# gMLP mixer of a fused encoder step: v turned into rows on VectorE and through DRAM instead of on TensorE, and weight chunks fetched one chunk further ahead

## Chip, cores, metric

One core of one Trainium2 chip runs the whole step in one launch. The metric is the device time of that launch in microseconds (us); the kernel before has a median of 1330.05 us.

## What is computed

Two layers of macaron form run on 256 prompt frames and 32 sample frames (288 columns in all), model width 1024. Every layer is half a SwiGLU feed-forward, a mixer, and half a feed-forward. The mixer of layer 1 is the chunked gMLP that the change touches:

```python
def _mixer_c(h, w_in, ln_g, ln_b, w_s, b_s, w_out):
    u, v = jnp.split(jax.nn.gelu(h @ w_in), 2, axis=-1)      # 2048 channels each
    v = _layernorm(v, ln_g, ln_b)                            # over the channels
    ...
    mixed = jnp.einsum('gij,bnjgc->bnigc', ws, vg) + b_s...  # over the 128 frames of a chunk, 8 groups
    return (u * mixed.reshape(B, T, D_C)) @ w_out, v
```

All operands are float32.

## The kernel before

**Layout.** Activations lie with channels on the partitions and the 288 frames along the free axis (32 sample frames first). The weights stream from DRAM as chunks of up to 1024 rows by 256 columns (1 MB), in the order in which they are used. `fetch` (L180) loads a chunk into one of three `wraw` buffers through SP's queue. `pieces` splits it in four pieces of two 128-row blocks: ScalarE casts the high part `wh` (L207) and VectorE subtracts to get the low part `wl` (L208). The `wh` and `wl` tiles hold four half chunks each, so a chunk is split while the chunk ahead of it multiplies. `mm` then runs, for each row block and each half of the 256 columns, three products of 288 columns (L247 with `wl`, L248 and L249 with `wh`): 48 products for a chunk of eight blocks. The first product of a block is the one that reads `wl`.

**Queues.** `next_chunk` issues the fetches ahead and `tick` hands out the pieces and the work of "lanes" (side work, at a rate per row block). The Tile layer then schedules: it may move an instruction later or earlier on its engine while the program is built, and what it leaves is a fixed order on each engine. On the chip every engine works through its own order; an instruction that waits holds up all behind it on that engine.

**The mixer, `mixer_c`.** Eight v chunks (called v0 to v7 here), then eight u chunks (u0 to u7), then the output projection in eight chunks (o0, o1, ...). A chunk's two accumulators are evacuated by VectorE (L296), which multiplies by the norm; the accumulators are two pairs, so the chunk after next needs the evacuation. ScalarE then applies the gelu (L992 and L994 for v, L1089 for u).

- `tokens(n, v)` turns a v chunk so that frames lie on the partitions: four 128x128 transposes on TensorE (L975) into PSUM and one copy by ScalarE (L976) into `vt`. After every second chunk the sample's part `vs` is turned too (L981, L982), and VectorE takes the statistics of 512 channels of `vt` (L984).
- `statistics` joins them (L1008 to L1016) and takes the power on GpSimd (L133). `normed` scales `vt` and `vs` in nine steps on VectorE (L1025).
- `spatial(n)` multiplies `vt` of chunk n by the spatial weights on TensorE (L1050 for the sample, L1069), finishes on VectorE (L1057 to L1082), and `put` writes the product with u as high part `hh` (ScalarE, L316) and low part `hl` (VectorE, L317). `u` has four buffers, so u4 can be evacuated only when u0 is done.
- The projection reads `hh` and `hl`: its first chunk o0 needs u0 to u3, o1 needs u4 to u7.

Of the kernel before, what the change touches and what calls it, by code (L numbers as in the profile page):

```python
# [14 lines left out]
P = 128  # L15
D = 1024
KD = D // P
TP = 256
TS = 32
# [12 lines left out]
WIN = ((32, 160), (160, 288), (0, 128))  # L32
# [61 lines left out]
class Net:  # L94
# [4 lines left out]
    def __init__(self, tc, ctx, I, O):  # L99
        self.tc, self.nc, self.I, self.O = tc, tc.nc, I, O  # L100
        e = ctx.enter_context
        self.const = e(tc.tile_pool(name="const", bufs=1))
        self.wraw = e(tc.tile_pool(name="wraw", bufs=3))
        self.wspl = e(tc.tile_pool(name="wspl", bufs=4))
        self.acc = e(tc.tile_pool(name="acc", bufs=2, space=PSUM))
        self.misc = e(tc.tile_pool(name="misc", bufs=4, space=PSUM))
        self.nrm = e(tc.tile_pool(name="nrm", bufs=1))
        self.stream, self.pos = [], 0
        self.raw, self.spl = {}, {}
        self.uid = 0  # L110
        self.ahead = None
        self.lanes = []
        self.lv = None
        self.nlane = Lane(self.NORM_RATE)
# [38 lines left out]
    def to_cols(self, name, b, x, xs):  # L153

        pt = self.ps(name)
        for i in range(2):
            self.nc.tensor.transpose(pt[:, i * P:i * P + P], x[:, i], self.ident)
        if b == 0:
            self.nc.tensor.transpose(pt[:, TP:TP + P], xs, self.ident)
        return pt  # L160

    def both(self, x):

# [48 lines left out]
    def next_chunk(self):  # L212
        i = self.pos
        self.pos += 1
        for _ in self.ahead or self.pieces(i):
            pass
        for j in (i + 1, i + 2):
            self.fetch(j)
        self.ahead = self.pieces(i + 1)
        self.rate = -(-self.blocks(i + 1) // self.PIECE) / self.blocks(i)  # L220
        self.due = 0.999
        self.raw.pop(i)
        return self.spl.pop(i)
# [686 lines left out]
    def mixer_c(self, gnext):  # L910
        nc, I, O = self.nc, self.I, self.O
# [3 lines left out]
        with self.tc.tile_pool(name="c", bufs=1, reuse_waits="tile") as pool:  # L915
            self.hidden(pool, 16)
            T = lambda tag, shape, bufs=None: self.t(pool, shape, tag, bufs=bufs)
# [4 lines left out]
            J = N // 2  # L922
            vt, vs, vc = T("vt", [P, 2, DC]), T("vs", [P, J, P]), T("vc", [P, J, P])
            st = T("st", [P, 3, 4, 6])
# [28 lines left out]
            def row_sums():  # L953
# [6 lines left out]
                for a, e in ((0, 3), (3, 6), (6, 8)):  # L960
# [4 lines left out]
                    nc.scalar.copy(out=rs[:, a:e], in_=pt[:, :n].rearrange("p (g i) -> p g i", i=P + TS))  # L965
                    yield

            def tokens(n, v):
                yield
                pv = self.ps("vt")  # L970
                for w in range(2):
                    for b in range(2):
                        s, e = WIN[w]
                        a = 256 * w + P * b
                        nc.tensor.transpose(pv[:, a:a + P], v[:, b, s:e], self.ident)  # L975
                nc.scalar.copy(out=vt[:, :, n * 256:n * 256 + 256], in_=pv.rearrange("p (w c) -> p w c", w=2))  # L976
                yield
                if n % 2:
                    j = n // 2
                    pv = self.ps("vs")  # L980
                    nc.tensor.transpose(pv[:, :P], vc[:, j], self.ident)  # L981
                    nc.scalar.copy(out=vs[:, j], in_=pv[:, :P])  # L982
                    for w in range(2):
                        nc.vector.bn_stats(st[:, w, j], vt[:, w, (n - 1) * 256:(n + 1) * 256])  # L984
                    yield

            spw = spatial_weights()
            next(spw)
# [14 lines left out]

            def statistics():
                mv = state["mv"] = T("mv", [P, 3, 2])

                sp = T("sp", [P, 6])
                nc.vector.bn_stats(sp, vs.rearrange("p j c -> p (j c)"))  # L1008
# [19 lines left out]

            def sample_out():

                gb, bb, y = (T(n, [P, J, P]) for n in ("lng", "lnb", "vo"))
                for to, name in ((gb, "c_ln_g"), (bb, "c_ln_b")):
                    for k in range(4):
                        nc.gpsimd.dma_start(out=to[TS * k:TS * k + TS], in_=I[name][0].rearrange(
# [334 lines left out]
```

## Time and profile before

| what | us |
|---|---|
| median of three runs (1329.81, 1330.05, 5818.11) | 1330.05 |
| the profiled execution | 1330.23 |
| its span, first to last instruction | 1328.5 |
| TensorE busy in it (PE) | 1322.6 |
| VectorE busy (DVE) | 878.4 |
| ScalarE busy (ACT) | 672.7 |

The profile follows one execution. PE is TensorE's products, PEld its weight loads, DVE VectorE, ACT ScalarE, POOL GpSimd, SP the engine that issues most transfers; a q behind a name is that engine's instruction queue. Lines (L247) are those of the kernel before. A product's duration is modelled and overlaps the next one, so the pace of TensorE is read from the starts. 1330.23 less 1328.5 leaves 1.7 us outside the span.

### The profile page before, as it was taken

How to read it: one execution, taken by the hardware profiler on the slowest of the kernel's cores; microseconds unless marked ns; L12 is line 12 of the kernel's file. 1: busy time of each engine (PE TensorE's matmuls, PEld its weight loads, DVE VectorE, ACT ScalarE, POOL GpSimd, SP SyncE). 2: the span in 40 equal slices, each digit the busy share in tenths (PEclk: the TensorE clock that was granted, in tenths of full speed). 3: DMA queues.
4: the chain of work that ended last, by engine and by line, in shares of the span. 5: the costliest groups of instructions: out<-in, count | busy, mean ns of one | idle time of the engine just before them, and what ended most of it. 6: DMA issues, size and time to landing. Idle time of an engine off the chain costs nothing.

```text
span 1328.5 us, 24573 instructions
## 1 busy us (share of the span) xinstructions
PE 1322.6 (100%) x9986; PEld 1316.6 (99%) x9986; DVE 878.4 (66%) x1682; ACT 672.7 (51%) x1381; POOL 43.6 (3%) x67
## 2 busy tenths in 40 slices
PE   9999999999999999999999999999999999999998
PEld 9999999999999999999999999999999999999998
DVE  7666556879787866666555766655568966665653
ACT  7544445474747466544444644444565445444432
POOL 1000000010111010000000000020000000000000
PEclk9999999999999999999999999999999999999999
DMA  8555455453544346555545555575544545555443
GB/s 282 178 178 168 144 175 186 154 161 108 165 135 136 113 135 199 159 159 162 175 148 183 159 169 167 173 191 178 164 155 131 163 159 159 164 167 178 151 129 105
DMA packets 221907, 214.70 MB, mean 162 GB/s; under 512 B 12385, under 2 KB 221074, under 8 KB 221794
## 3 DMA queue, kind: packets, MB, share of 16 engines
q1 hardware_dynamic: 221010, 211.20, 50.7%
q0 software_dynamic: 624, 1.77, 0.6%
q8 instruction: 78, 1.28, 0.4%
q14 instruction: 35, 0.29, 0.1%
q10 hardware_dynamic: 160, 0.17, 0.1%
HBM read 208.27 MB, written 4.85 MB: 160 GB/s over the span
## 4 chain that ended last, share of the span: by engine, by line
PE 98%; DMA 1%; DVE 0%; SPq 0%; issue 0%; ACT 0%; DVEq 0%
PE acc L249 30%; PE acc L248 30%; PE acc L247 30%; PE sc L612 1%; DMA wraw<-in_ffn_w_up_dram 1%; PE sp L1069 1%; PE S L685 0%; PE zs L822 0%; PE sc L640 0%; PE ob L889 0%; PE vt L975 0%; PE kt L141 0%; PE z L834 0%; PE ob L884 0%; DVE wl L208 0%; SPq L190 0%
## 5 line engine op out<-in xcount | busy, mean ns | idle before, releaser
L207 ACT CAST wh<-wraw 128x512 fp32r<-128x512 f32 x768 | 441.9, 619 | 475.6 <-PE acc L249 358.3
L208 DVE TENSOR_TENSOR wl<-wraw,wh 128x512 fp32r<-128x512 f32 x768 | 508.0, 688 | 260.9 <-ACT wh L207 260.1
L247 PE MATMUL acc<-xh,wl 128*128 128x288 f32 x2096 | 629.1, 300 | 0.0
L249 PE MATMUL acc<-xh,wh 128*128 128x288 f32 x2096 | 618.6, 295 | 0.0
L248 PE MATMUL acc<-xl,wh 128*128 128x288 f32 x2096 | 618.5, 295 | 0.0
L248 PEld LDWEIGHTS acc<-xl,wh 128*128 128x128 f32 x2096 | 394.1, 188 | 0.5
L247 PEld LDWEIGHTS acc<-xh,wl 128*128 128x128 f32 x2096 | 393.9, 188 | 0.6
L249 PEld LDWEIGHTS acc<-xh,wh 128*128 128x128 f32 x2096 | 393.5, 188 | 0.0
L247 PE MATMUL acc<-hh,wl 128*128 128x288 f32 x960 | 284.7, 297 | 0.0
L248 PE MATMUL acc<-hl,wh 128*128 128x288 f32 x960 | 283.4, 295 | 0.0
L249 PE MATMUL acc<-hh,wh 128*128 128x288 f32 x960 | 283.1, 295 | 0.0
L247 PEld LDWEIGHTS acc<-hh,wl 128*128 128x128 f32 x960 | 180.2, 188 | 0.8 <-ACT hh L866 0.2
L248 PEld LDWEIGHTS acc<-hl,wh 128*128 128x128 f32 x960 | 180.3, 188 | 0.2
L249 PEld LDWEIGHTS acc<-hh,wh 128*128 128x128 f32 x960 | 180.3, 188 | 0.0
L296 DVE TENSOR_TENSOR u<-acc,rb 128x576 f32<-128x576 f32 x52 | 39.4, 757 | 49.1 <-PE acc L249 49.1
L296 DVE TENSOR_TENSOR g<-acc,rb 128x576 f32<-128x576 f32 x47 | 35.6, 758 | 46.6 <-PE acc L249 46.6
L316 ACT CAST hh<-u 128x576 fp32r<-128x576 f32 x52 | 35.1, 676 | 55.2 <-DVE u L442 40.4
L317 DVE TENSOR_TENSOR hl<-u,hh 128x576 fp32r<-128x576 f32 x52 | 39.4, 759 | 7.7 <-ACT hh L316 1.7
L323 ACT ACTIVATE xh<-xT,cols 128x288 fp32r<-128x288 f32 x40 | 21.3, 532 | 26.5 <-DVE xT L391 15.4
L442 DVE TENSOR_TENSOR u<-u,g 128x576 f32<-128x576 f32 x44 | 33.1, 753 | 0.0
L440 ACT ACTIVATE g<-g 128x576 f32<-128x576 f32 x44 | 30.0, 681 | 0.1
L324 DVE SCALAR_TENSOR_TENSOR xl<-xT,cols,xh 128x288 fp32r<-128x288 f32 x40 | 20.6, 516 | 8.5 <-ACT xh L323 8.5
(315 smaller groups left out, 777.6 us busy)
## 6 DMA issues: line engine op xcount, KB each, us to landing
wraw<-in_ffn_w_up_dram SPq DMA_DIRECT2D x44, 1024.0 KB, 6.0
wraw<-in_ffn_w_gate_dram SPq DMA_DIRECT2D x43, 1024.0 KB, 5.4
wraw<-in_ffn_w_down_dram SPq DMA_DIRECT2D x32, 1024.0 KB, 5.3
wraw<-in_ab_w_in_dram SPq DMA_DIRECT2D x28, 1024.0 KB, 5.2
wraw<-in_c_w_in_dram SPq DMA_DIRECT2D x16, 1024.0 KB, 5.4
wraw<-in_ffn_w_down_dram SPq DMA_DIRECT2D x16, 768.0 KB, 4.5
wraw<-in_c_w_out_dram SPq DMA_DIRECT2D x8, 1024.0 KB, 5.3
wraw<-in_ab_w_out_dram SPq DMA_DIRECT2D x8, 768.0 KB, 4.4
```

What stands on the lines that cost most here:

```text
L207: self.nc.scalar.copy(out=h[:, x], in_=w[:, a:b])
L208: self.nc.vector.tensor_tensor(out=l[:, x], in0=w[:, a:b], in1=h[:, x].bitcast(F32), op=ALU.subtract)
L247: mm(o, lhsT=l[:, k, c], rhs=hi[:, r], start=st, stop=False)
L248: mm(o, lhsT=h[:, k, c], rhs=lo[:, r], start=False, stop=False)
L249: mm(o, lhsT=h[:, k, c], rhs=hi[:, r], start=False, stop=en)
L296: self.nc.vector.tensor_tensor(out=x, in0=acc[:, :, :NT], in1=self.rb, op=ALU.mult)
L316: nc.scalar.copy(out=hh, in_=h)
L317: nc.vector.tensor_tensor(out=self.hl[:, k:k + 2], in0=h, in1=hh.bitcast(F32), op=ALU.subtract)
L323: nc.scalar.activation(out=self.xh[:, k], in_=x, func=AF.Copy, scale=g)
L324: nc.vector.scalar_tensor_tensor(out=self.xl[:, k], in0=x, scalar=g, in1=self.xh[:, k].bitcast(F32), op0=ALU.mult, op1=ALU.subtract)
L440: nc.scalar.activation(out=g, in_=g, func=AF.Silu)
L442: nc.vector.tensor_tensor(out=u, in0=u, in1=g, op=ALU.mult)
```

## The change

The transposes of a v chunk leave TensorE. VectorE transposes blocks of 32x32 inside two instructions of 128x256 per chunk, into a tile of 128x512 that shares a buffer with `lnb` or `vo`. Four transfers (one for each 32 partitions) write it to a scratch in DRAM in runs of 32 floats, which puts the blocks in their places; two transfers read it back into `vt`, 128x2x128 each. ScalarE's copy goes away. The statistics of 512 channels are taken one chunk later (the last in `statistics`). `next_chunk` also fetches chunk i + 3; `wraw` still has three buffers.

```diff
@@ class Net
+        self.rows = e(tc.tile_pool(name="rows", bufs=2, space=bass.MemoryType.DRAM))
...
+    def to_rows(self, y, x):
+
+        nc = self.nc
+        n = y.shape[1]
+        for i, e in x:
+            nc.vector.transpose(y[:, i:i + e.shape[1]], e)
+        rows = self.t(self.rows, [n, P], "rows")
+        to = rows.rearrange("(n t) (a c) -> a t n c", t=TS, a=4)
+        for q in range(4):
+            nc.sync.dma_start(out=to[q], in_=y[TS * q:TS * q + TS].rearrange("t (n c) -> t n c", c=TS))
+        return rows
...
-        for j in (i + 1, i + 2):
+        for j in (i + 1, i + 2, i + 3):
             self.fetch(j)
@@ mixer_c
+            def means(j):
+                for w in range(2):
+                    nc.vector.bn_stats(st[:, w, j], vt[:, w, 512 * j:512 * j + 512])
+
             def tokens(n, v):
                 yield
-                pv = self.ps("vt")
-                for w in range(2):
-                    for b in range(2):
-                        s, e = WIN[w]
-                        a = 256 * w + P * b
-                        nc.tensor.transpose(pv[:, a:a + P], v[:, b, s:e], self.ident)
-                nc.scalar.copy(out=vt[:, :, n * 256:n * 256 + 256], in_=pv.rearrange("p (w c) -> p w c", w=2))
+                y = T(("lnb", "vo")[n % 2], [P, 2 * TP])
+                rows = self.to_rows(y, [(TP * b, v[:, b, TS:]) for b in range(2)])
+                for b in range(2):
+                    c = n * 256 + b * P
+                    nc.sync.dma_start(out=vt[:, :, c:c + P],
+                                      in_=rows[TP * b:TP * b + TP].rearrange("(w t) c -> t w c", t=P))
                 yield
                 if n % 2:
...
-                    for w in range(2):
-                        nc.vector.bn_stats(st[:, w, j], vt[:, w, (n - 1) * 256:(n + 1) * 256])
-                    yield
+                elif n:
+                    means(n // 2 - 1)
+                yield
...
             def statistics():
                 mv = state["mv"] = T("mv", [P, 3, 2])
+                means(J - 1)
```

The orders below are those of the built programs; lines of the changed kernel are shifted (L309 is the old L296, L220 and L221 are L207 and L208, L1106 is L1089, L330 is L317, L1093 is L1076, L1098 is L1081). Numbers behind a name tell one buffer's use from another.

**Place 1, VectorE from the evacuation of u1 to that of u3.** `wraw_11616` is u3's chunk before, `wraw_11550` after; `wraw_11709` and `wraw_11642` are u4's. Before, with the evacuations of u1 (`acc_11615`) and u2 (`acc_11708`):

```order
L208 TENSOR_TENSOR wl_11718<-wraw_11616,wh_11717 128x512
L1025 TENSOR_SCALAR vt_10878<-vt_10878,mv_11653,pw_11668 128x512 x2
L1025 TENSOR_SCALAR vs_10879<-vs_10879,mv_11653,pw_11668 128x512
L1025 TENSOR_SCALAR vt_10878<-vt_10878,mv_11653,pw_11668 128x512 x2
L296 TENSOR_TENSOR u_11705<-acc_11615,rb_10942 128x576
L1025 TENSOR_SCALAR vt_10878<-vt_10878,mv_11653,pw_11668 128x512 x4
L208 TENSOR_TENSOR wl_11752<-wraw_11616,wh_11751 128x512 x2
L208 TENSOR_TENSOR wl_11803<-wraw_11709,wh_11802 128x512
L1059 TENSOR_TENSOR xs_11764<-sp_11761,cols 128x128
```

After, with the evacuations of u2 (`acc_11739`) and u3 (`acc_11814`):

```order
L309 TENSOR_TENSOR u_11811<-acc_11739,rb_10946 128x576
L168 STREAM_TRANSPOSE vo_11674<-v_11545 128x256 x2
L221 TENSOR_TENSOR wl_11749<-wraw_11550,wh_11748 128x512
L983 BN_STATS st_10885<-vt_10882 128x6 x2
L221 TENSOR_TENSOR wl_11749<-wraw_11550,wh_11748 128x512
L221 TENSOR_TENSOR wl_11784<-wraw_11550,wh_11783 128x512 x2
L309 TENSOR_TENSOR u_11902<-acc_11814,rb_10946 128x576
L221 TENSOR_TENSOR wl_11824<-wraw_11642,wh_11823 128x512 x2
L221 TENSOR_TENSOR wl_11869<-wraw_11642,wh_11868 128x512 x2
L221 TENSOR_TENSOR wl_11915<-wraw_11740,wh_11914 128x512
L983 BN_STATS st_10885<-vt_10882 128x6 x2
```

The split of u3's chunk stood ahead of u2's evacuation and stands behind it now, all four pieces; the split of u4's chunk stands behind u3's evacuation. The transposes of v7 and the last statistics stand there as well.

**Place 1, ScalarE, from the gelu of u0.** Before:

```order
L1089 ACTIVATE u_11601<-u_11601 128x576
L207 CAST wh_11676<-wraw_11527 128x512
L982 COPY vs_10879<-vs_11634 128x128
L207 CAST wh_11717<-wraw_11616 128x512 x2
L207 CAST wh_11751<-wraw_11616 128x512 x2
L1089 ACTIVATE u_11705<-u_11705 128x576
L207 CAST wh_11802<-wraw_11709 128x512 x2
```

After:

```order
L1106 ACTIVATE u_11627<-u_11627 128x576
L220 CAST wh_11690<-wraw_11461 128x512
L998 COPY vs_10883<-vs_11700 128x128
L1106 ACTIVATE u_11736<-u_11736 128x576
L1106 ACTIVATE u_11811<-u_11811 128x576
L220 CAST wh_11748<-wraw_11550 128x512 x2
L220 CAST wh_11783<-wraw_11550 128x512 x2
L1106 ACTIVATE u_11902<-u_11902 128x576
L220 CAST wh_11823<-wraw_11642 128x512 x2
```

The casts of u3's chunk stood ahead of the gelu of u1 and stand behind the gelu of u2 now, those of u4's behind the gelu of u3.

**Place 2, TensorE, the first spatial product.** Before it stands in chunk u2 (`acc_11708`), 36 products into it:

```order
L248 MATMUL acc_11708<-xl,wh_11676 128x288
L249 MATMUL acc_11708<-xh,wh_11676 128x288
L1050 MATMUL sp_11761<-wsB_10886,vs_10879 128x128
L247 MATMUL acc_11708<-xh,wl_11677 128x288
L248 MATMUL acc_11708<-xl,wh_11676 128x288
```

After it stands in chunk u5 (`acc_11994`), 22 products into it, with three more behind it:

```order
L260 MATMUL acc_11994<-xh,wl_11915 128x288
L1067 MATMUL sp_11833<-wsB_10890,vs_10883 128x128
L1086 MATMUL sp_11856<-wsT_10889,vt_10882 128x128 x2
L1086 MATMUL sp_11878<-wsT_10889,vt_10882 128x128 x2
L1086 MATMUL sp_11945<-wsT_10889,vt_10882 128x128 x2
L261 MATMUL acc_11994<-xl,wh_11914 128x288
```

The spatial products of all eight u chunks are moved towards the end of the stage by nearly three chunks.

**Place 2, VectorE, around the last `hl` of the stage.** Before, with u6's (`u_12150`) and u7's (`u_12237`); `wl_12398` is half of o1's first chunk:

```order
L317 TENSOR_TENSOR hl_10877<-u_12150,hh_10876 128x576
L1076 SCALAR_TENSOR_TENSOR x_12328<-sp_12329,cols,z_12332 128x256
L1076 SCALAR_TENSOR_TENSOR x_12328<-sp_12335,cols,z_12338 128x256
L208 TENSOR_TENSOR wl_12398<-wraw_12241,wh_12397 128x512
L1081 TENSOR_TENSOR u_12237<-x_12328,u_12237 128x2x256
L208 TENSOR_TENSOR wl_12398<-wraw_12241,wh_12397 128x512
L317 TENSOR_TENSOR hl_10877<-u_12237,hh_10876 128x576
```

After, with u6's (`u_12173`) and u7's (`u_12263`); `wl_12416` is the first half of o1's first chunk:

```order
L330 TENSOR_TENSOR hl_10881<-u_12173,hh_10880 128x576
L1093 SCALAR_TENSOR_TENSOR x_12364<-sp_12371,cols,z_12374 128x256
L1099 TENSOR_TENSOR u_12263<-xs_12328,u_12263 128x2x32
L1098 TENSOR_TENSOR u_12263<-x_12364,u_12263 128x2x256
L221 TENSOR_TENSOR wl_12416<-wraw_12177,wh_12415 128x512 x2
L330 TENSOR_TENSOR hl_10881<-u_12263,hh_10880 128x576
```

The rows here are much the same as before. Those of all eight u chunks lie between the first spatial product and this place, in a shorter stretch of the program now.

**Place 3, SP's queue around the last rows.** Before, the fetches of u4 to u6 (`wraw_11709` and the two behind it) follow each other with nothing between:

```order
L180 DMA wraw_11616<-in_c_w_in_dram 128x8x256
L180 DMA wraw_11709<-in_c_w_in_dram 128x8x256
L180 DMA wraw_11794<-in_c_w_in_dram 128x8x256
L180 DMA wraw_11883<-in_c_w_in_dram 128x8x256
L1040 DMA out_dram<-vo_11606 128x1x128 x4
```

After (`rows_11604` is v6, `rows_11677` v7; `wraw_11642` is u4's chunk, `wraw_11740` u5's):

```order
L172 DMA rows_11604<-lnb_11601 32x16x32 x4
L193 DMA wraw_11642<-in_c_w_in_dram 128x8x256
L991 DMA vt_10882<-rows_11604 128x2x128 x2
L172 DMA rows_11677<-vo_11674 32x16x32 x4
L193 DMA wraw_11740<-in_c_w_in_dram 128x8x256
L991 DMA vt_10882<-rows_11677 128x2x128 x2
L193 DMA wraw_11815<-in_c_w_in_dram 128x8x256
```

Between two fetches there are now four writes to the scratch and two reads from it, and a read waits for its writes to land. Outside the mixer the orders of TensorE, VectorE, ScalarE and GpSimd are the same rows; on SP a fetch is moved ahead of a small transfer in a few places.

## Rows read from the trace of the kernel before

**Rows 1.** The page: busy time, share and instructions of the engines.

```profile
PE 1322.6 (100%) x9986; PEld 1316.6 (99%) x9986; DVE 878.4 (66%) x1682; ACT 672.7 (51%) x1381; POOL 43.6 (3%) x67
```

**Rows 2.** The page, the chain that ended last: shares by engine.

```profile
PE 98%; DMA 1%; DVE 0%; SPq 0%; issue 0%; ACT 0%; DVEq 0%
```

**Rows 3.** What TensorE's products waited for over the whole span, the longest of them: total us, times, longest.

```profile
PE acc L1144 <- DVE ms L1155: 1.2, 1, 1.2
```

**Rows 4.** TensorE's products in order of time around one set of transposes: start us, us, engine, line, operation, count.

```profile
961.98 0.29 PE L249 MATMUL acc<-xh,wh 128*128 128x288 f32 x1
962.11 0.60 PE L975 MATMUL vt<-ident,v 128*128 128x128 f32 x4
962.47 0.38 PE L247 MATMUL acc<-xh,wl 128*128 128x288 f32 x1
962.68 0.30 PE L248 MATMUL acc<-xl,wh 128*128 128x288 f32 x1
962.82 0.29 PE L249 MATMUL acc<-xh,wh 128*128 128x288 f32 x1
```

**Rows 5.** The weight loads around the first set: the same columns, and in brackets the idle time and what ended it.

```profile
958.03 0.42 PEld L975 LDWEIGHTS vt<-ident,v 128*128 128x128 f32 x4 [0.26 <-ACT v L994]
```

**Rows 6.** VectorE in order of time: u0's evacuation, a stretch of the u chunks, and the last `hl`; columns as in rows 4 and 5. The pace is read from start to start.

```profile
1008.74 0.76 DVE L296 TENSOR_TENSOR u<-acc,rb 128x576 f32<-128x576 f32 x1 [1.24 <-PE acc L249]
...
1019.30 1.91 DVE L1025 TENSOR_SCALAR vt<-vt,mv,pw 128x512 f32<-128x512 f32 x4
1021.12 1.90 DVE L208 TENSOR_TENSOR wl<-wraw,wh 128x512 fp32r<-128x512 f32 x3
1022.93 0.29 DVE L1059 TENSOR_TENSOR xs<-sp,cols 128x128 f32<-128x128 f32 x1
...
1030.25 0.77 DVE L317 TENSOR_TENSOR hl<-u,hh 128x576 fp32r<-128x576 f32 x1
1030.92 0.24 DVE L1082 TENSOR_TENSOR u<-xs,u 128x64 f32<-128x64 f32 x1
1031.05 0.30 DVE L1057 TENSOR_TENSOR zs<-RS,cols 128x128 f32<-128x128 f32 x1
1031.25 0.77 DVE L296 TENSOR_TENSOR u<-acc,rb 128x576 f32<-128x576 f32 x1
1031.92 0.50 DVE L1076 SCALAR_TENSOR_TENSOR x<-sp,cols,z 128x256 f32<-128x256 f32 x1
1032.31 0.70 DVE L208 TENSOR_TENSOR wl<-wraw,wh 128x512 fp32r<-128x512 f32 x1
...
1034.11 0.36 DVE L1073 SCALAR_TENSOR_TENSOR z<-RS,cols,BS 128x128 f32<-128x128 f32 x1
1034.37 0.70 DVE L1081 TENSOR_TENSOR u<-x,u 128x512 f32<-128x512 f32 x1
1034.97 0.37 DVE L1073 SCALAR_TENSOR_TENSOR z<-RS,cols,BS 128x128 f32<-128x128 f32 x1
...
1071.29 0.76 DVE L317 TENSOR_TENSOR hl<-u,hh 128x576 fp32r<-128x576 f32 x1 [0.20 <-ACT hh L316]
```

**Rows 7.** ScalarE, GpSimd and VectorE, groups by line and form from 950 to 1085 us: count | busy us, mean ns of one | idle time ahead of them.

```profile
L207 ACT CAST wh<-wraw 128x512 fp32r<-128x512 f32 x76 | 44.3, 618 | 28.7 <-PE acc L249 22.0 <-issue 6.6
L1089 ACT ACTIVATE u<-u 128x576 f32<-128x576 f32 x8 | 5.5, 686 | 8.5 <-DVE u L296 8.5
...
L133 POOL TENSOR_TENSOR pw<-ve,mhalf 128x3 f32<-128x3 f32 x1 | 1.2, 1244 | 124.8 <-DVE ve L1016 124.8
...
L984 DVE BATCH_NORM_STATS2 st<-vt 128x6 f32<-128x512 f32 x8 | 5.1, 682 | 0.7 <-ACT vt L976 0.7
...
L1012 DVE BATCH_NORM_AGGREGATE mv<-st 128x2 f32<-128x24 f32 x3 | 0.6, 236 | 0.0
```

**Rows 8.** TensorE in order of time, the product that the last `hl` lets start; columns as in rows 4.

```profile
1071.95 0.29 PE L247 MATMUL acc<-hh,wl 128*128 128x288 f32 x1
1072.10 0.40 PE L248 MATMUL acc<-hl,wh 128*128 128x288 f32 x1
```

**Rows 9.** VectorE's transposes of the results (L1307): duration in ns, least, median and most.

```profile
L1307 DVE STREAM_TRANSPOSE sq<-xT x6: 472/472/478, 1269.5 to 1308.8; 128x288 f32<-128x288 f32 x6
```

**Rows 10.** SP's own time to issue the transfers of the results (L1311) and of one output tile (L1040): ns, least, median, most.

```profile
L1311 SPq DMA_DIRECT2D out_dram<-sq x48: 314/434/1401, 1270.0 to 1314.8; - x48
...
L1040 SPq DMA_DIRECT2D out_dram<-vo x4: 588/600/707, 1027.1 to 1029.1; - x4
```

**Rows 11.** Transfers by issue: count, KB each, median us from issue to landing.

```profile
wraw<-in_c_w_in_dram SPq DMA_DIRECT2D x16, 1024.0 KB, 5.4
...
out_dram<-sq SPq DMA_DIRECT2D x24, 32.0 KB, 2.4
```

**Rows 12.** Two windows: length, then busy us (instructions) of PE, PEld, DVE, ACT, POOL, the granted clock, the DMA share and GB/s. The first holds small writes of results alone, the second weight fetches.

```profile
1290.00:1295.00 5.00, 5.00 (x40) 5.00 (x39) 3.30 (x6) 1.46 (x3) 0.00 (x0) 1.00 0.23 37
941.00:947.40 6.40, 6.40 (x51) 6.40 (x50) 4.75 (x9) 4.42 (x10) 0.00 (x0) 1.00 0.53 164
```

**Rows 13.** What SP's queue waited for over the whole span: total us, times, longest.

```profile
SPq L180 <- DVE wl L208: 970.1, 171, 11.0
```

**Rows 14.** Two windows, columns as in rows 12: one of the v chunks, one of the u chunks.

```profile
981.00:987.50 6.50, 6.50 (x51) 6.50 (x50) 3.38 (x6) 3.04 (x7) 0.00 (x0) 1.00 0.55 164
1022.00:1029.00 7.00, 7.00 (x56) 7.00 (x55) 7.00 (x16) 3.32 (x6) 0.00 (x0) 1.00 0.54 163
```

More of the change, by code (lines that the diff above doesn't have):

```diff
@@ L1029, in sample_out @@
             def sample_out():
-                gb, bb, y = (T(n, [P, J, P]) for n in ("lng", "lnb", "vo"))
+                gb, bb, y = (T(n, [P, J * P]).rearrange("p (j c) -> p j c", c=P) for n in ("lng", "lnb", "vo"))
                 for to, name in ((gb, "c_ln_g"), (bb, "c_ln_b")):
```

## Prediction

> **What bounds the kernel now.** I read the page's busy time first: TensorE is busy 1322.6 us [rows 1], all but 6 us of the span. The chain that ended last is TensorE's to 98% [rows 2], and the longest thing that a product waited for cost 1.2 us, once [rows 3]. So TensorE sets the time, without a gap. A microsecond taken off it is gained, and any time in which it waits is lost, since nothing behind it has slack to give back. The pace is read from starts: in a run of products they lie 0.13 us apart, and a chunk of 48 takes 6.4 us.
>
> **What TensorE gains.** Around one set of four transposes, products start at 961.98 and, three products later, at 962.82 [rows 4]. Three steps alone are 0.40, so a set costs 0.44 us. Eight sets are 3.5, and the first made the weight loads wait 0.26 for the gelu [rows 5]: 3.8 us in all. Of these, 3.3 us (seven sets and the wait) lie ahead of the end of u0, which is at 1008.74 (its evacuation starts there [rows 6]). ScalarE loses eight copies; it does not set the time.
>
> **What the new order costs.** An engine runs its rows in the order that was built, so I walk place 1 with durations of before. Let T be the end of u2's products. u1 and u2 are 12.8 us and u1 holds one small transpose (0.1), so T = 1008.74 - 3.3 + 12.9 = 1018.3.
>
> *u3 and u4.* The split of u3 stands behind u2's evacuation now. TensorE, done with u2, waits for the evacuation (0.76 [rows 6]), the gelu behind it on ScalarE (0.69), a cast (0.62 [rows 7]) and a subtract (0.70 [rows 6]): 2.8 us, with nothing else to multiply, since its own order has u3 next. The other pieces come every 0.6 us, apart from two statistics of 0.6 us each (0.68 long [rows 7], overlapping) between the first and second, which make a block wait about 0.3 more. u3 ends at T + 9.5. The same chain stands ahead of u4: 2.8 us again, first product at T + 12.2, end at T + 18.6. Before, both splits were done while the chunk ahead multiplied.
>
> *The statistics.* VectorE goes on from u3's evacuation: 0.7, a wait of 1.3 for gelu and cast, five subtracts (3.0, from 1021.12 to 1022.93 for three [rows 6]) to T + 14.6; two statistics 1.2, two joins of 0.24 [rows 7], two subtracts 1.2 and a small row to T + 17.6; GpSimd's power 1.24 [rows 7], with hand-offs 1.5, to T + 19.1; nine scalings at 0.455 (1019.30 to 1021.12 for four [rows 6]) to T + 23.2. Nothing of the spatial work can start on VectorE before that. u5 has its weights by then, and its first spatial product stands 22 products in.
>
> *The run on VectorE.* From T + 23.2 to the last `hl` (place 2) the order holds 92 rows on VectorE: 16 of L1076 at 0.39, 8 of L1081 at 0.60, 8 of L1082 at 0.13, 14 of L1073 at 0.26, 14 for xs and zs (L1057 to L1060) at 0.20, 2 for the output tile at 0.60, 8 `hl` and 4 evacuations at 0.67, and 18 subtracts at 0.60 (from starts in [rows 6]; the output tile's rows have the subtract's size). That is 6.2 + 4.8 + 1.0 + 3.6 + 2.8 + 1.2 + 8.0 + 10.8 = 38.4 us. In the walk what they read from TensorE is there earlier, and each `hl` stands at least 0.8 us behind the row that its cast reads, about what a cast takes. So VectorE runs without a gap and the last `hl` ends near T + 61.6 = 1079.9. Before, it ended at 1071.29 + 0.76 = 1072.05 [rows 6], and the product that reads it started at 1072.10, 0.15 behind the one ahead [rows 8]: VectorE and TensorE met there without slack. That is 7.9 us later.
>
> *TensorE's own sum* agrees. It waits 3.1 us at u3 and 2.8 at u4. It is done with u5 by T + 28.9 (48 products, and spatial sets, each as long as a set of transposes, that wait for VectorE to free their buffers), and u6's first subtract ends at T + 30.3: 1.4. It then stays just behind VectorE's subtracts until the first weights of o1, which end 1.3 us ahead of the last `hl`, at T + 60.4; it is there by T + 56.1: 4.3. Together 11.6; less the 3.3 gained, it comes 8.3 us later to the same product. I take **8.1 us later**. From there both programs hold the same rows, and TensorE has no slack to catch up with.
>
> **What I cost at nothing.** *The transposes on VectorE.* The trace has one of 128x288 at 472 ns [rows 9]; by size, 128x256 is 0.42, and 16 are 6.7 us. In a v chunk VectorE is busy 3.4 of 6.5 us [rows 14], in another stretch 4.75 of 6.4 [rows 12], and 0.84 more fits in either. Without that cover they would cost 6.7.
>
> *The way through DRAM.* Only v7's rows can matter. They are transposed by T + 1.6, written by four issues of 0.43 to 0.60 on SP [rows 10], and land 2.4 us later as other small writes do [rows 11], near T + 6.2. The reads stand behind u5's fetch, 1 MB in 5.4 us [rows 11], and land by T + 10.5; VectorE asks for them at T + 14.6. That is 4 us of cover. The price of 128 B pieces: results moved at 37 GB/s for 5 us with a share of 0.23 [rows 12], 185 KB in pieces of 128 B, so 18.4 engine-us over 1450 pieces, 13 ns each. Weight fetches move 164 KB a us in 1 KB rows for 0.53 of 16 engines [rows 12], 52 ns each. So 2048 pieces of a v chunk take 1.6 us of the 16 engines, or 6.6 if a piece is as dear as 1 KB. The upper end eats the cover and costs 1 us. The share is 0.55 in a v chunk [rows 14], so 1.6 of 6.5 us fit and 6.6 do not. I take the lower, since it is read from pieces of the same size.
>
> A rule stands against this route. The Trainium skill ("DMA: Bandwidth & Descriptors", Specifications) says that transfers under 512 B fall short of line rate because the engine reads and modifies what it writes. By the trace a 128 B piece moves 10 bytes per ns against 20 for 1 KB, so half the rate agrees with it, and the sum is the same by either.
>
> *The fetch one further ahead.* SP's queue waits 970.1 us, 171 times, for a subtract to free a buffer [rows 13]. There are still three buffers, so a fetch issued earlier waits at the same place; what could change is a small transfer caught behind it.
>
> **Sum.** The profiled execution of before is 1330.23, within 0.2 of the median 1330.05. 1330.05 + 8.1 = **1338 us**.
>
> **Rivals.**
>
> *A, faster: the order costs nothing.* If rows of place 1 do not wait as I read them (the splits are ready in time), only the gain is left: 1330.05 - 3.8 = 1326. For it: in the v chunks and before, splits were always ready, and TensorE never waited. Against: a row cannot pass the one ahead of it on its engine, and the gelu of u2 needs u2's last product. It decides when the waits at u3 and u4 sum to under 3.8 instead of 5.9 and the run on VectorE is shorter by as much. A mixture ends between 1326 and 1338.
>
> *B, slower: the rows come late.* If reads of v7 land after T + 14.6, every microsecond over moves the whole run. With pieces at 52 ns, v7's rows, written and read behind v6's (13 us of the 16 engines) and a fetch (5.4), land at T + 3.6 + 18.8 = T + 22, some 7 us too late: 1345; with u5's weights late by as much as a fetch, 1350. For it: four writes, a fetch and two reads stand in one queue, and a read waits for writes to land with all behind it. Against: the 13 ns.
>
> *C, slower: the clock.* All windows of before have a granted clock of 1.00 [rows 12, 14], the 2.4 GHz level, with TensorE never idle over 1.2 us. Now it waits 2.8 and 4.4 us. If the clock fell to 1.2 GHz at u3 and stayed so for u3 and u4, their 12.8 us would take 25.6; VectorE's run hangs on u3's end alone, 6.4 later, and u4's lies beside it: 1345 to 1351. If it stayed to the last `hl`, TensorE's 45 us of products would be 90 and VectorE no longer the bound: near 1370. Against: no window of before shows it. The Trainium skill ("TensorE: Matmul & The Clock Gate", HAM oscillation) tells of kernels whose bursts between waits ran at the lower clock; no run here shows that yet.
>
> *D, the part that does nothing.* If the fetch order does move a buffer's arrival, no product waits for one in the stretch before [rows 3], so it has nothing to save: 1338 stays.
>
> **How the numbers follow.** My forecast (8.1 later, 1331 to 1346 by mistakes of one wait of 2.8, or of a tenth of the run, to either side) has 0.66 with D in it, A 0.14, B 0.13, C 0.07. The range 1326 to 1352 takes in A's end and most of B, and leaves some 0.15 out. About 2% is what a measurement of this kernel can tell from no change: 1303.4 to 1356.7. Nothing in the profile gives over 3.8 us, so faster has 0.01. Slower needs the worse half of C and the tail of B, 0.08. The rest, 0.91, is the same.
>
> **What would show it.** In the profile after: no transposes inside the v chunks, starts 0.13 apart through them; waits of TensorE of about 2.8 us for a subtract at the first products of u3 and u4; scalings that start near 1037; VectorE without a gap from there to a last `hl` near 1080; a wait of some 4 us for o1's first weights. It is wrong if those two waits are missing (A), if VectorE waits for a read at the statistics (B), or if a window there has a granted clock under 1 (C).

## The result, and the profile after

The changed kernel takes 1344.76 us (median of six runs, 1340.94 to 1345.79), the one before 1330.14: a ratio of 1.0107, 95% interval [1.0097, 1.0117]. The profiled execution took 1345.76, its span 1344.0, so the same 1.7 us lie outside. The forecast was 1338 in a range of 1326 to 1352, and 0.91 for a change within 2%. The time lies in the range and on the forecast's side, and the slowdown of 1.1% is clear of the interval, but the loss of 14.6 us is nearly twice the 8.1 that was worked out.

The page of the changed kernel, busy time of the engines and the chain's shares, beside [rows 1, 2]:

```profile
PE 1328.0 (99%) x9954; PEld 1321.0 (98%) x9954; DVE 883.4 (66%) x1698; ACT 667.9 (50%) x1373; POOL 43.7 (3%) x67
...
PE 22%; DVE 1%; ACT 0%; issue 0%; DVEq 0%
```

TensorE is no longer busy without a gap: 16 us of its span are free now, against 6. The chain, 98% TensorE before, can be followed back through less than a quarter of the span and passes VectorE and ScalarE on the way. What its products waited for (total us, times, longest), beside [rows 3]:

```profile
PE acc L260 <- DVE wl L221: 7.2, 4, 2.9
PE acc L260 <- ACT hh L329: 2.9, 1, 2.9
```

VectorE in order of time (L309 is the evacuation, L168 the transposes, L221 a subtract, L983 statistics, L1042 a scaling, L330 an `hl`), beside [rows 6]:

```profile
954.90 0.75 DVE L309 TENSOR_TENSOR v<-acc,rb 128x576 f32<-128x576 f32 x1
...
1005.70 0.76 DVE L309 TENSOR_TENSOR u<-acc,rb 128x576 f32<-128x576 f32 x1 [2.55 <-PE acc L262]
...
1018.55 0.76 DVE L309 TENSOR_TENSOR u<-acc,rb 128x576 f32<-128x576 f32 x1 [3.95 <-PE acc L262]
1019.23 0.76 DVE L168 STREAM_TRANSPOSE vo<-v 128x256 f32<-128x256 f32 x2
1020.57 0.69 DVE L221 TENSOR_TENSOR wl<-wraw,wh 128x512 fp32r<-128x512 f32 x1 [0.58 <-ACT wh L220]
...
1030.81 0.76 DVE L309 TENSOR_TENSOR u<-acc,rb 128x576 f32<-128x576 f32 x1 [6.55 <-PE acc L262]
1032.82 3.10 DVE L221 TENSOR_TENSOR wl<-wraw,wh 128x512 fp32r<-128x512 f32 x5 [1.26 <-ACT wh L220]
1035.84 1.28 DVE L983 BATCH_NORM_STATS2 st<-vt 128x6 f32<-128x512 f32 x2
...
1039.98 1.00 DVE L1042 TENSOR_SCALAR vt<-vt,mv,pw 128x512 f32<-128x512 f32 x2 [0.78 <-POOL pw L134]
...
1084.52 0.75 DVE L330 TENSOR_TENSOR hl<-u,hh 128x576 fp32r<-128x576 f32 x1
```

The first row is the evacuation of v0, ahead of all transposes. Before, it stands here:

```profile
954.61 0.75 DVE L296 TENSOR_TENSOR v<-acc,rb 128x576 f32<-128x576 f32 x1
```

So this execution is 0.3 us late before the change can act. From v0's evacuation to u0's (1005.70 against 1008.74) it takes 50.80 us, against 54.13: the transposes that left TensorE are worth 3.3 us up to there, as worked out. u2's evacuation starts at 1018.55 (T was put at 1018.3). Behind it stand the two transposes of v7, and the first subtract for u3 starts only at 1020.57, released by a cast that itself stood behind the gelu of u2. The same at u4: evacuation at 1030.81, subtract at 1032.82.

TensorE's products at these places (start us, us, line, in brackets the idle time and what ended it), beside [rows 8]:

```profile
1021.41 0.58 PE L260 MATMUL acc<-xh,wl 128*128 128x288 f32 x1 [2.89 <-DVE wl L221]
1021.78 0.44 PE L261 MATMUL acc<-xl,wh 128*128 128x288 f32 x1
1022.02 0.44 PE L262 MATMUL acc<-xh,wh 128*128 128x288 f32 x1
...
1033.66 0.37 PE L260 MATMUL acc<-xh,wl 128*128 128x288 f32 x1 [2.89 <-DVE wl L221]
...
1081.50 0.41 PE L260 MATMUL acc<-hh,wl 128*128 128x288 f32 x1 [2.88 <-ACT hh L329]
1082.33 0.61 PE L261 MATMUL acc<-hl,wh 128*128 128x288 f32 x1 [0.42 <-DVE hl L330]
```

The first product of u3 waited 2.89 us, that of u4 the same, and the third stall, in front of the last `hl`, was 2.88 for the `hh` of u6 and 0.42 for its `hl`. The second thing to see is the pace behind a wait: products start 0.24 us apart (1021.78, 1022.02) where they start 0.13 apart before ([rows 4]). The windows say why. Their granted clock is the share of TensorE's full clock that the chip let through in the stretch (length, busy us of PE, PEld, DVE, ACT, POOL with counts, the granted clock, DMA share, GB/s), beside [rows 12, 14]:

```profile
985.00:1005.00 20.00, 20.00 (x151) 19.89 (x150) 12.65 (x23) 11.30 (x24) 0.00 (x0) 1.00 0.67 180
1021.30:1027.50 6.20, 6.09 (x25) 6.12 (x26) 2.96 (x5) 0.80 (x2) 0.00 (x0) 0.50 0.99 255
1034.00:1037.20 3.20, 3.20 (x17) 3.20 (x16) 3.20 (x7) 2.43 (x5) 0.00 (x0) 0.56 0.20 44
1082.90:1089.00 6.10, 5.84 (x25) 5.53 (x24) 4.03 (x7) 1.06 (x2) 0.00 (x0) 0.50 0.24 61
1089.00:1092.00 3.00, 3.00 (x25) 3.00 (x24) 0.75 (x2) 1.37 (x4) 0.00 (x0) 1.00 0.65 228
```

Behind the wait at u3 the granted clock is 0.50, the 1.2 GHz level, for some 6 us; behind the one at u4 products start 0.24 apart from about 0.8 us after the first one until 1037.7, some 3 us (0.56 over the window); behind the third it is 0.50 for 6 us again, and 1.00 from 1089 on. The Trainium skill ("TensorE: Matmul & The Clock Gate", HAM oscillation) describes this: bursts of products between waits run at the lower clock. This trace agrees, with 0.50 to 0.56 behind these three waits of 2.9 us; a run below shows such waits without a fall.

The transposes on VectorE (duration in ns, least, median and most), and, from L991's answer, the time from issue to landing of the reads from the scratch (us):

```profile
L168 DVE STREAM_TRANSPOSE lnb<-v x8: 401/421/446, 958.3 to 1012.2; 128x256 f32<-128x256 f32 x8
...
DMA to landing us min/median/max: 4.3/4.7/5.2
```

0.42 us each, as worked out by size from [rows 9]. In the v chunks (985 to 1005 in the windows above) TensorE is busy 20.00 of 20 us at clock 1.00 with all of this beside it.

### The profile page after: what moved, and what is told of

It reads as the page before. It is cut to its first block, busy times and chain, and to the rows that moved or that the text cites. A ratio compares the mean times of both kernels' runs of the same rounds, so it can differ in the third digit from the quotient of the medians.

```text
span 1344.0 us, 24633 instructions
## 1 busy us (share of the span) xinstructions
PE 1328.0 (99%) x9954; PEld 1321.0 (98%) x9954; DVE 883.4 (66%) x1698; ACT 667.9 (50%) x1373; POOL 43.7 (3%) x67
## 2 busy tenths in 40 slices
DMA packets 243156, 218.91 MB, mean 163 GB/s; under 512 B 29537, under 2 KB 242322, under 8 KB 243042
## 5 line engine op out<-in xcount | busy, mean ns | idle before, releaser
L220 ACT CAST wh<-wraw 128x512 fp32r<-128x512 f32 x768 | 440.7, 618 | 475.2 <-PE acc L262 367.2
L221 DVE TENSOR_TENSOR wl<-wraw,wh 128x512 fp32r<-128x512 f32 x768 | 506.5, 687 | 251.2 <-ACT wh L220 250.3
L309 DVE TENSOR_TENSOR u<-acc,rb 128x576 f32<-128x576 f32 x52 | 39.4, 757 | 61.0 <-PE acc L262 60.9
L309 DVE TENSOR_TENSOR g<-acc,rb 128x576 f32<-128x576 f32 x47 | 35.6, 757 | 46.6 <-PE acc L262 46.6
L330 DVE TENSOR_TENSOR hl<-u,hh 128x576 fp32r<-128x576 f32 x52 | 39.4, 758 | 6.7 <-ACT hh L329 0.9
```

What stands on the lines that cost most here:

```text
L220: self.nc.scalar.copy(out=h[:, x], in_=w[:, a:b])
L221: self.nc.vector.tensor_tensor(out=l[:, x], in0=w[:, a:b], in1=h[:, x].bitcast(F32), op=ALU.subtract)
L309: self.nc.vector.tensor_tensor(out=x, in0=acc[:, :, :NT], in1=self.rb, op=ALU.mult)
L330: nc.vector.tensor_tensor(out=self.hl[:, k:k + 2], in0=h, in1=hh.bitcast(F32), op=ALU.subtract)
```

## The experiments

Theory 1: the loss is the built order (splits behind evacuations, and VectorE's late run to the last `hl`), and on top of it the clock, which falls in the waits that the order makes. Theory 2: the way through DRAM costs the time, by its pieces of 128 bytes, late rows or other transfers held up. Ratios are to runs of the kernel before on the same chip, where its medians are 1329.83 to 1330.23; the changed kernel's 1344.76 is from the result above.

**The fetch alone, on the kernel before (e1_ahead_only).**

```diff
-        for j in (i + 1, i + 2):
+        for j in (i + 1, i + 2, i + 3):
```

> The kernel before with the fetch of chunk i + 3 alone: transposes on TensorE, no scratch. Theory 1 (the changed kernel loses its time because the splits of u3 and u4 stand behind evacuations in the built order, and because TensorE's clock falls in the waits that follow): in this kernel the splits stand ahead of the evacuations, so no wait, granted clock 1.00, 1330 us within 1. Rival (a fetch put earlier into SP's queue costs something by itself, whatever the order): 1334 or more.

1330.36 us, ratio 1.0002 [0.9993, 1.0011], clock 1.00, TensorE's longest wait the 1.2 us of [rows 3]. With three buffers the extra fetch does nothing by itself.

**The changed kernel without the fetch (e2_no_ahead).**

```diff
-        for j in (i + 1, i + 2, i + 3):
+        for j in (i + 1, i + 2):
```

> The changed kernel without the fetch of chunk i + 3; transposes on VectorE and the way through DRAM stay as they are, on SP's queue. In its built order the split of u3 stands ahead of u2's evacuation and that of u4 ahead of u3's, and the first spatial product is one chunk earlier. Theory 1: no waits of 2.8 us at u3 and u4, clock 1.00 through u7, last hl between 1070 and 1076, time 1326 to 1333. Rival (theory 2: the way through DRAM costs the time, by 128-byte pieces, late rows or other transfers held up on SP's queue): the route is the same here, so 1340 or more.

1352.64 us, ratio 1.0174 [1.0157, 1.0191]: 7.9 us slower than with the fetch, and in the rival's range. The expectation was wrong, and so was my reading of the order: I had taken chunks' buffers for those of one chunk further on. The split of u2 stands behind u1's evacuation here, u3's behind u2's, u4's behind u3's, and another such place lies among the v chunks. TensorE's weight loads (start us, us, idle time in brackets) show the four:

```profile
996.10 0.19 PEld L260 LDWEIGHTS acc<-xh,wl 128*128 128x128 f32 x1 [3.11 <-issue]
...
1020.95 0.29 PEld L260 LDWEIGHTS acc<-xh,wl 128*128 128x128 f32 x1 [4.08 <-issue]
...
1031.78 0.19 PEld L260 LDWEIGHTS acc<-xh,wl 128*128 128x128 f32 x1 [3.10 <-issue]
...
1041.28 0.29 PEld L260 LDWEIGHTS acc<-xh,wl 128*128 128x128 f32 x1 [3.10 <-issue]
```

So this run does not part the two theories as it was meant to. What it shows is that the fetch one further ahead, worth nothing in the kernel before, is worth 7.9 us beside the new transfers: without it two more chunks' splits fall behind an evacuation (one among the v chunks, and u2's).

**The six transfers of a v chunk on GpSimd (e3_rows_pool).**

```diff
-            nc.sync.dma_start(out=to[q], in_=y[...
+            nc.gpsimd.dma_start(out=to[q], in_=y[...
...
-                    nc.sync.dma_start(out=vt[:, :, c:c + P],
+                    nc.gpsimd.dma_start(out=vt[:, :, c:c + P],
```

In this run, in e7 and in e8 the writes of the results (L1328), which are written the same way, went to GpSimd too; in e4 to ScalarE.

> The changed kernel with the six transfers of a v chunk (four writes to the scratch, two reads) issued by GpSimd instead of SP; the fetch one further ahead stays. The built order has half of each split ahead of the evacuation and half behind, the scalings right behind u3's evacuation. Theory 1: no wait at u3 and u4, clock 1.00, the gain of 3.8 us on TensorE shows: 1326 to 1331. Theory 2 (the pieces of 128 bytes are what costs): the same pieces, so 1340 or more. If GpSimd's own issue is slow, the rows land later and the statistics of v7 wait: up to 1336.

1330.16 us, ratio 1.0002 [0.9993, 1.0012]. The same rows go through DRAM, behind the same transposes, and 14.6 us are gone: the waits at u3 and u4 do not exist, and the clock is 1.00 through the u chunks. That is theory 1's range. It does not exclude theory 2 by itself, since on GpSimd's queue the page counts other packets:

```profile
DMA packets 217556, 218.91 MB, mean 165 GB/s; under 512 B 6625, under 2 KB 215314, under 8 KB 217442
```

Under 512 B there are 6625, against 29537 in the changed kernel and 12385 in the kernel before. What a piece of 128 bytes costs inside a larger packet no run shows. What speaks against theory 2 is the changed kernel's own trace: between 950 and 1090 us all waits of VectorE and ScalarE for a transfer sum to 0.2 us, and TensorE's stalls go back to evacuation, gelu, cast and subtract.

The gain of 3.8 does not show. VectorE's first scaling, its last `hl`, and the weight loads around it:

```profile
1026.83 1.00 DVE L1042 TENSOR_SCALAR vt<-vt,mv,pw 128x512 f32<-128x512 f32 x2 [0.78 <-POOL pw L134]
...
1069.56 0.75 DVE L330 TENSOR_TENSOR hl<-u,hh 128x576 fp32r<-128x576 f32 x1
...
1066.54 0.19 PEld L260 LDWEIGHTS acc<-hh,wl 128*128 128x128 f32 x1 [1.43 <-ACT hh L329]
1067.37 0.19 PEld L261 LDWEIGHTS acc<-hl,wh 128*128 128x128 f32 x1 [0.64 <-DVE hl L330]
...
1069.16 0.50 PEld L260 LDWEIGHTS acc<-hh,wl 128*128 128x128 f32 x2 [1.10 <-issue]
```

The scalings start at 1026.83, against 1016.35 before, so VectorE's run still ends as its last `hl` does at 1069.56 + 0.75 = 1070.3; TensorE, 3 us earlier here, waits 1.43, 0.64 and 1.10 for it. Behind the last of these waits its granted clock is 0.63 from 1068.1 to 1072.0. The two together take the gain back.

**The six transfers on ScalarE (e4_rows_act).** The same edit with `nc.scalar`.

> The changed kernel with the six transfers of a v chunk issued by ScalarE instead of SP. The built order has the splits ahead of the evacuations. Theory 1: 1326 to 1331 if ScalarE's waits for the writes to land (some 2.4 us ahead of each pair of reads) stay hidden; if they hold up the casts behind them, TensorE waits up to 2 us at a chunk and the time is 1332 to 1340. Theory 2: 1340 or more with no new wait of TensorE for a cast.

1341.82 us, ratio 1.0088 [1.0073, 1.0103]. ScalarE around one pair of reads, and the weight load that waited (the last line):

```profile
974.18 0.91 ACTq L991 DMA_DIRECT2D vt<-rows  x2
975.12 0.61 ACT L962 COPY wsB<-wsT 32x128 f32<-32x128 f32 x2 [3.34 <-issue]
...
974.68 0.19 PEld L260 LDWEIGHTS acc<-xh,wl 128*128 128x128 f32 x1 [3.15 <-issue]
```

The engine's next copy starts at 975.12, 3.34 us idle, since the two reads in front of it were issued only at 974.18, when the writes had landed (the four in front were issued from 967.08 and took 5.3 us by their median). The casts behind wait with it, and TensorE for them, 3.15 us. That is theory 1's second branch, larger than expected: waits of up to 3.15 instead of 2 us, six waits of products for a subtract with 10.4 us in all, and a time 1.8 us over the branch's range. A queue that waits for a landing must not be one on which something urgent stands.

**Products of no use in the three waits (e5_fill).** 20, 22 and 28 products into a spare accumulator; VectorE's order is row by row that of the changed kernel.

```diff
+            def fill(k, p=None, x=None):
+                p = self.ps("fill") if p is None else p
+                for i in range(k):
+                    r = self.xh[:, i % KD] if x is None else x
+                    mm(p[:, :r.shape[1]], lhsT=self.onr, rhs=r, start=i == 0, stop=i == k - 1)
...
             for n in range(N):
+                if n == 3:
+                    fp = self.ps("fill")
+                    fill(20, fp)
+                if n == 4:
+                    fill(22, fp, self.used[1][1][:, 3])
                 u = self.evac(pool, "u", self.C_LAG + 1)
...
             lane.drain()
             self.lanes = []
+            fill(28)
```

> The changed kernel with products of no use put into TensorE's three long waits: 20 ahead of u3, 22 ahead of u4, 28 in front of o1's first weights (into a spare accumulator that nothing reads). VectorE's order is the changed kernel's, row by row. Theory 1, its second half (the clock falls in these waits and takes the 6 us by which the changed kernel lies above the forecast): with TensorE busy there the granted clock stays 1.00 and the time falls to the sum of the forecast, 1337 to 1340. Rival (the extra 6 us are waits for data or order that I did not see): the time stays at 1344 to 1346, or rises by the added work.

1339.3 us (1338.61 to 1339.34), ratio 1.0069 [1.0054, 1.0084]: 5.5 us faster than the changed kernel, by adding work. The windows at u3 and behind the last `hl`, columns as above:

```profile
1022.00:1030.00 8.00, 8.00 (x64) 7.89 (x63) 2.80 (x6) 1.29 (x3) 0.00 (x0) 1.00 1.01 294
1080.00:1090.00 10.00, 10.00 (x78) 10.00 (x77) 7.80 (x15) 4.96 (x10) 0.00 (x0) 1.00 0.39 118
```

The clock is 1.00 in them, and VectorE's steps come at the times of the forecast:

```profile
1018.28 0.76 DVE L309 TENSOR_TENSOR u<-acc,rb 128x576 f32<-128x576 f32 x1 [3.95 <-PE acc L262]
...
1037.10 1.01 DVE L1042 TENSOR_SCALAR vt<-vt,mv,pw 128x512 f32<-128x512 f32 x2 [0.78 <-POOL pw L134]
...
1080.16 0.75 DVE L330 TENSOR_TENSOR hl<-u,hh 128x576 fp32r<-128x576 f32 x1
```

u2's evacuation at 1018.28 (forecast 1018.3), scalings from 1037.10 (1037.4), last `hl` done by 1080.9 (1079.9). This settles the clock's share: about 5.5 of the 14.6 us. The rest, 9.2, is the sum that was worked out as 8.1. The added products take little themselves: the product that reads the last `hl` starts at 1081.22, 0.3 us behind it.

**The lane's rate at 0.8, transfers on SP (e6_rate).**

```diff
-    C_RATE = 0.5
+    C_RATE = 0.8
```

> The changed kernel with the lane's rate at 0.8 in place of 0.5, so that the rows, the statistics and the spatial steps are handed out earlier; transfers stay on SP. In its built order the splits of u2, u3 and u4 each stand behind the evacuation ahead, and the last hl comes more than a chunk earlier in the program. Theory 1: three waits of 2.8 to 3.1 us at u2, u3 and u4 with the clock falling behind some of them, but no wait in front of o1's weights: 1335 to 1344. Rival (late rows make TensorE wait, and the order does not matter): earlier rows, fewer waits, under 1333.

1346.3 us, ratio 1.0122 [1.0105, 1.0139], 2 us over the expected range's upper end. The three waits are there at the chunks that the order names, and no wait in front of o1:

```profile
1014.74 0.19 PEld L260 LDWEIGHTS acc<-xh,wl 128*128 128x128 f32 x1 [3.10 <-issue]
...
1024.37 0.29 PEld L260 LDWEIGHTS acc<-xh,wl 128*128 128x128 f32 x1 [3.09 <-issue]
...
1036.51 0.19 PEld L260 LDWEIGHTS acc<-xh,wl 128*128 128x128 f32 x1 [3.09 <-issue]
```

The clock behind the first of them, and behind the second:

```profile
1014.90:1021.00 6.10, 6.10 (x46) 5.99 (x47) 2.72 (x5) 0.56 (x2) 0.04 (x1) 1.00 1.13 293
...
1024.50:1033.00 8.50, 8.50 (x45) 8.50 (x46) 1.56 (x3) 0.59 (x2) 0.00 (x0) 0.66 0.55 174
```

1.00 and 0.66, behind waits of 3.10 and 3.09 us. What was not expected is that the spatial products, which now stand early, waited another 3.2 us in all for VectorE. So earlier rows alone do not help while the transfers sit on SP's queue.

**GpSimd, and the sample output's fetches moved behind the rows (e7_rows_pool_late_ln).**

```diff
                     out = sample_out()
+                if n == 2:
                     next(out)
+                    lane.todo.append(out)
                 lane.todo.append(spatial(n))
-                if n == 0:
-                    lane.todo.append(out)
```

> The kernel with the six transfers on GpSimd, and the fetches for the sample's output (which stood between the writes of v7's rows on GpSimd) moved behind them, to u2. The statistics of v7 then stand right behind u2's evacuation. Theory 1 (what was left in the run on GpSimd is VectorE's late start: scalings 10 us later than before, so the last hl late): scalings begin 4 us earlier or more, no wait at the last hl, 1326 to 1328. Rival (128-byte pieces or GpSimd's issues hold it at 1330): 1329.5 to 1331.

1328.8 us, ratio 0.9991 [0.9982, 1.0000]: between the two ranges, 0.8 over theory 1's. The scalings came 1.5 us earlier than in e3, not 4, and VectorE now waits for the rows themselves:

```profile
1021.52 1.29 DVE L983 BATCH_NORM_STATS2 st<-vt 128x6 f32<-128x512 f32 x2 [1.21 <-DMA vt<-rows]
...
1025.30 1.00 DVE L1042 TENSOR_SCALAR vt<-vt,mv,pw 128x512 f32<-128x512 f32 x2 [1.00 <-POOL pw L134]
```

**The same with the lane's rate at 0.8 (e8_rows_pool_rate), and without the results' writes on GpSimd at 0.55 (e9_best55) and 0.6 (e10_best60).** The edits are e7's and a `C_RATE` of 0.8, 0.55 and 0.6.

> As the run before, and the lane's rate at 0.8: rows, statistics and spatial steps are handed out earlier still; every split stands ahead of the evacuation that its chunk waits behind. Theory 1: no wait of TensorE in the mixer, clock 1.00 throughout, the whole gain of 3.8 us: 1326 to 1327. Rival: as before, 1329.5 or more.

1329.79 us, ratio 0.9999 [0.9990, 1.0008]: missed, and in the rival's range. In the profiled execution (1328.93) the clock is 1.00, but TensorE waits, for VectorE to free the buffers of the spatial products that now stand early in its order:

```profile
1035.92 0.52 PEld L1086 LDWEIGHTS sp<-wsT,vt 128*128 128x128 f32 x4 [1.60 <-DVE xs L1076]
```

The ten executions fall into two groups: five of 1328.48 to 1329.31 with a mean granted clock of 0.999 to 1.000, and five of 1330.27 to 1330.60 with 0.998 to 0.999. So in half of them the clock takes its part too.

> The six transfers of a v chunk on GpSimd (the results' writes stay on SP here), the sample output's fetches behind the rows, the lane's rate at 0.55. The rate decides when spatial products stand in TensorE's order against the scalings on VectorE. Theory 1: the gain on TensorE is 3.8 us less the waits that are left; with spatial sets spread further than at 0.8, waits sum to under 1.5 us: 1326.3 to 1328.0. Rival (the gain itself is smaller than 3.8, some 1.3 as at 0.8): 1328.5 to 1329.5 with waits of under 0.5 us in the mixer.

1328.66 us, ratio 0.9989 [0.9980, 0.9997]: the lowest median (e7's is not told apart from it), and under the kernel before, by 1.6 us. Its waits in the mixer sum to 1.9 us:

```profile
1026.79 0.30 PEld L1067 LDWEIGHTS sp<-wsB,vs 128*128 128x128 f32 x2 [0.24 <-issue]
...
1035.53 0.19 PEld L260 LDWEIGHTS acc<-xh,wl 128*128 128x128 f32 x1 [0.33 <-DVE u L309]
...
1069.10 0.19 PEld L260 LDWEIGHTS acc<-hh,wl 128*128 128x128 f32 x1 [1.00 <-ACT hh L329]
1069.61 0.19 PEld L260 LDWEIGHTS acc<-hh,wl 128*128 128x128 f32 x1 [0.32 <-issue]
```

1330.2 - 3.8 + 1.9 = 1328.3, within 0.4 of the measured time. The waits were over the 1.5 that I had expected, and the time lies in the rival's range; but the rival's waits of under 0.5 us are not there, and from v0's evacuation to u0's (955.20 to 1006.00) the gain is the full 3.3 of theory 1.

> As the run before with the rate at 0.6: more spatial sets stand early in u4, so TensorE waits more for VectorE to free their buffers: theory 1 gives 1327 to 1329, the time being 1326.3 and the waits. Rival: 1328.5 to 1329.5 without waits.

1329.26 us, ratio 0.9996 [0.9986, 1.0005], 0.3 over theory 1's range and not told apart from before; it waits 1.60 us once for a spatial buffer, as at 0.8.

## Why the forecast's side was right and its size too small

**The gain on TensorE, 3.8 us:** right. Up to u0 it is 3.3, as worked out. The whole of it shows in the four runs in whose profiles the clock stays up. Take the span before, 1328.5, less 3.8, add the waits of the weight loads in the mixer, and the time by which v0's evacuation is later than before in that execution: e7 1328.5 - 3.8 + 2.6 + 0.0 = 1327.3 (measured 1327.2), e8 with 2.7 and -0.3 1327.1 (1327.2), e9 with 1.9 and 0.6 1327.2 (1327.2), e10 with 2.5 and -0.3 1326.9 (1326.9).

**The waits of TensorE, 3.1, 2.8, 1.4 and 4.3 us:** right. On the weight loads of the changed kernel they are 3.10 at u3, 3.10 at u4, 1.31 at u6 and 4.33 around the last `hl` (3.12, 0.64 and 0.57): 11.8 in all, against 11.6. The last was forecast in front of o1's first weights; most of it came a little earlier, at the `hh` of u6. T, the chain of evacuation, gelu, cast and subtract, and VectorE's way to the scalings came out within 0.3 us in e5, where VectorE's order is that of the changed kernel and the clock stays up. One slip in the sum: it took off the 3.3 gained up to u0, but by the last `hl` all 3.8 are gained, so TensorE's own sum is 7.8 and not 8.3.

**VectorE's run to the last `hl`, 42.5 us from the first scaling:** it took 43.8 in e5 (1037.10 to 1080.9) and 45.3 in the changed kernel (1039.98 to 1085.3). The step that each `hl` never waits for its `hh` was too kind: in e5 `hl` waited twice, 0.7 us in all. That is the larger part of the 1 us by which e5's last `hl`, and its time, lie over the forecast (1339.3 against 1338.1). Of the other 1.5 in the changed kernel, 0.9 are waits for the first spatial products, which TensorE reached late behind the slow stretch in u4.

**What failed in size is the clock.** The sum held TensorE at 2.4 GHz through all three waits; the lower clock stood only as rival C, with 0.07. In the profiled execution the waits of 11.8 less the gain of 3.8, with the 0.3 of the late start, leave 8.3, and the span is 15.5 longer than before. The missing part is the pace: some 24 products behind u3's wait, 14 in u4 and 25 behind the last wait start 0.24 us apart instead of 0.133, and 63 times 0.107 is 6.7. e5, without them, is 5.5 faster by the medians and 6.5 by the spans of the profiled executions (1344.0 and 1337.5; that of the changed kernel lies 1.0 over its median). C's own case was the fall at u3 and u4 without a recovery, 1345 to 1351; the clock came back after 6, 3 and 6 us, and it fell a third time, so C's number was near for the wrong place. That 1344.8 lies in the forecast's own band (1331 to 1346) is in part luck: the band was meant for waits or a run of a wrong size, and what filled it was the clock.

**What was costed at nothing was nothing.** The transposes took 0.42 us each, in time that VectorE had. The rows of v7 were read by two transfers issued from 1023.89 that land in 4.3 to 5.2 us, some 1029, as worked out (T + 10.5 = 1028.8), and VectorE asked for them at 1035.84. Rival B did not come, and its 52 ns a piece is not the price. In e4 ScalarE's queue carries these transfers and the results' writes (packets, MB, share of 16 engines):

```profile
q10 hardware_dynamic: 29088, 5.25, 2.1%
```

2.1% of 16 engines over a span of 1339.0 us is 450 engine-us, 15 ns a packet, near the 13 that were read. (The 1.6 us for a v chunk counted the writes alone; the reads back, 512 pieces of 512 B, were left out.) The Trainium skill ("DMA: Bandwidth & Descriptors", Specifications) has transfers under 512 B short of line rate, and this queue agrees: 12 bytes per ns, against 20 for the 1 KB rows of the weights [rows 12]. It cost the changed kernel nothing, as nothing waited for these transfers but 0.2 us. Where other engines issued the rows, VectorE did wait for them once: 1.21 us in e7 and 0.73 in e4. The fetch ahead costs and gains nothing in the kernel before (e1); that it is worth 7.9 us in the changed one (e2) I had not seen, since I weighed it only against the old order. Rival A (the order costs nothing) is excluded by the two waits.

Left open: why the scheduling layer places the splits behind the evacuations when the transfers stand on SP. The order of SP's queue, where a fetch stands behind writes that wait for VectorE's transposes, and the cure by another queue (e3) suggest it (between 950 and 1045 us SP's queue waits 17 us with the writes for VectorE's transposes, and 8.5 with the reads for the writes), but what the layer counts was not examined.

## What to carry to other kernels

Transfers that wait for other engines belong on a queue on which nothing urgent stands behind them; here the kernel with these transfers loses 14.6 us when they stand on SP's, 11.7 on ScalarE's, and nothing on GpSimd's. Read the built order, not the diff: what a change removes on the busy engine (3.8 us) is small beside what a moved row on another engine can cost. And price a new wait on TensorE with two terms: its length, and the products behind it if the clock falls, which here was more than half as much again (about 5.5 us for 9.1 us of waits at three places).

## What the hardware showed beyond that

The clock does not fall behind every wait of the same length. The idle time of the products is 2.89 us in front of u3 in the changed kernel and in front of u2 and u3 in e6 (3.10 and 3.09 on e6's weight loads). Behind the first the granted clock was 0.50; in e6 it stayed 1.00 for the 6.1 us shown behind one, and was 0.66 over the 8.5 us behind the other.

Nor does it fall as often in every execution of the same program. The changed kernel's six executions spread over 4.9 us (1340.94 to 1345.79): the one of 1340.94 has a mean granted clock of 0.997, the other five (1344.03 and more) 0.994 or 0.995. In e3 the two of 1332.1 have 0.997, the other eight (1328.8 to 1330.4) 0.998 to 1.000. The executions of e5, whose clock stays up (0.999 to 1.000), spread over 0.7. Where in the program the clock fell is known for the profiled executions alone.
